# Beginning the block sums' transfers from GpSimd's queue, in a hybrid attention layer

## The chip, the cores and the metric

The kernel runs on one core of a Trainium2 chip. A core has TensorE (PE; its weight loads are listed as PEld), VectorE (DVE), ScalarE (ACT), GpSimd (POOL) and SyncE (SP), and 16 DMA engines that move data between HBM and the on-chip memory. Each engine works through its own instructions in order. A transfer is begun by an instruction that stands in the queue of one of the engines; that instruction waits there for its semaphores, and so does everything behind it on that engine. The metric is the device time of one execution in microseconds (us).

## The reference

One layer over 1024 tokens of width 1024, all in float32. A normalised input is projected to the columns of three mixers: a gated delta rule in both directions, grouped-query attention (8 query heads, 2 key heads) and cross-attention into 256 memory tokens (4 heads). Each mixer is projected, multiplied by a sigmoid gate and summed; an output projection and a squared-ReLU MLP follow.

```
y_att = block_gqa(aq, ak, av)
y_x = cross_attention(x_q, mk, mv)
merged = jnp.sum(gates * yb, axis=2)
x = x + merged @ w_out[l]
x = x + jnp.square(jax.nn.relu(hf @ w_up[l])) @ w_down[l]
return rms_norm(x, final_norm_w)
```

## The kernel before

The MLP's two products are done as Strassen-like sets of seven block products (P1 to P7). For the second one the kernel needs, beside blocks of `w_down`, four sums of blocks of it for each of 16 row pairs. It makes them early, in the attention stage, and keeps them in HBM in `wt_d[0..15]`, 128x4x512 each; they are read again only in the last stage (P6, P7, P4, P5).

The attention stage is a loop over 64 tiles `t` of 128 queries. Its TensorE order is pinned, so TensorE takes every product exactly in the order written. One pass of the loop does the scores of tile `t+2`, sometimes the output product of a pair (`q_out`), one step of the cross-attention generator `cross()`, some gate products as filling (`fill`), the turning of the probabilities (`q_trans`), and one call `block_sums(t // 4, t % 4)`.

`block_sums` fills a tile `wc` (128x4x128, two buffers in the pool `wcp`) by two loads from `w_down`, makes four subtractions on GpSimd in place (L1031), and stores the tile to `wt_d` by one transfer. There are 64 calls: 128 loads of 128 KB, 256 subtractions, 64 stores of 256 KB.

`cross()` goes through four heads, 16 passes each. A head begins by four loads into `mkv`, its keys and values; `mkv` has one buffer, so the loads must wait for the last product of the head before, which reads it. Two passes later TensorE needs it for the scores of the new head.

`ld` (L97) is the helper that begins a transfer from SyncE's queue; nearly every transfer of the kernel goes through it. The order in each queue is set by a scheduler, not by the order in which the code is written. Behind the attention come the rest of the gate products and the merge of the three branches, in the order 0, 2, 1: for the second and third of them GpSimd adds into `g_acc` (L1116), after VectorE has made the product in `g_l` (L1115). `g_l` has two buffers, loaded through SyncE's queue.

Of the kernel before, what the change touches and what calls it, by code (L numbers as in the profile page):

```python
# [86 lines left out]
def hybrid_block(tc, x, mem, mix_norm_w, w_in, dn_conv_w, dn_a_log, dn_dt_bias, dn_norm_w, q_norm_w, k_norm_w,  # L87
                 mem_norm_w, w_mem_kv, w_branch, w_out, ffn_norm_w, w_up, w_down, final_norm_w, ca_d, cb_d, rope_d,
                 out, dbg=None):
    nc = tc.nc  # L90
    pe, act, dve, gp = TensorE(tc), nc.scalar, nc.vector, nc.gpsimd
    def ld(out, in_):
        if out.dtype == F32R:
            out = out.bitcast(F32)
        if in_.dtype == F32R:
            in_ = in_.bitcast(F32)
        return nc.sync.dma_start(out=out, in_=in_)  # L97
# [100 lines left out]
    wt_d = [dram.tile([P, 4, 512], F32, name=f"wt_d{k}") for k in range(16)]  # L198
# [825 lines left out]
    def block_sums(k, c):  # L1024
        cs = slice(c * P, (c + 1) * P)
        w = wcp.tile([P, 4, P], F32, name="wc", tag="wc")
        for j in range(2):
            src = w_down[(2 * k + j) * P:(2 * k + j + 1) * P].rearrange("p (h c) -> p h c", h=2)
            ld(out=w[:, 2 * j:2 * j + 2], in_=src[:, :, cs])
        for o, a, b in ((0, 1, 0), (1, 3, 1), (3, 3, 0), (2, 2, 3)):  # L1030
            gp.tensor_tensor(out=w[:, o], in0=w[:, a], in1=w[:, b], op=ALU.subtract)  # L1031
        ld(out=wt_d[k][:, :, cs], in_=w)

    cr = cross()
    fill(24 * GATES[0])
# [7 lines left out]
    for t in range(NT):  # L1043
        if t + 2 < NT:
            q_scores(t + 2)
        if t % 2 == 0 and t:
            q_out(t // 2 - 1)
        next(cr, None)
        fill(FILL[0])
        q_trans(t, 0)  # L1050
        block_sums(t // 4, t % 4)
        fill(FILL[1])
        q_trans(t, 1)
        fill(FILL[2])
# [372 lines left out]
```

## Time and profile before

| | before |
|---|---|
| median of 3 runs | 1926.17 us (1922.19 to 1927.29) |
| the profiled execution's own time | 1923.72 us |
| its span in the profile | 1921.9 us |
| TensorE busy in the span | 1827.6 us (95%) |
| GpSimd busy | 532.4 us (28%) |
| packets of SyncE's DMA queue | 51.8% of 16 engines' span |

The span runs from the first to the last instruction seen; the execution's own time is 1.8 us longer. Busy shares are means over stages with different limits, so what a change in one stage does is to be read in that stage: the attention loop lies between about 588 and 1018 us.

### The profile page before, as it was taken

To read this page: it belongs to the slowest core of one execution; us is meant where nothing else is said; L and a number is where in the kernel's file an instruction comes from. 1 tells how busy PE (TensorE), PEld (TensorE's weight loads), DVE (VectorE), ACT (ScalarE), POOL (GpSimd) and SP (SyncE) were. 2 spreads that over 40 slices of the span, in tenths; PEclk is the share of its full clock that TensorE was granted. 3 is DMA by queue.
4 is the path that set the end of the run, shared out by engine and by line. 5 is a ranking of instruction groups with operands and counts; after the bars stand their busy time and mean duration, and the time that the engine had idled before them with its cause. 6 is when DMAs were issued, how large, how long until landed. Compare 5 with 4: busy or idle time off the path is not lost.

```text
span 1921.9 us, 27229 instructions
## 1 busy us (share of the span) xinstructions
PE 1827.6 (95%) x9891; PEld 1546.2 (80%) x9891; DVE 1237.4 (64%) x1795; ACT 808.2 (42%) x1597; POOL 532.4 (28%) x598
## 2 busy tenths in 40 slices
PE   6999999999999959869999999989999999999998
PEld 5888788988988848758888887867888888788886
DVE  4677989993676636646663456367787776555562
ACT  5453434653545636546663113133222223543341
POOL 1003131231343434442000052123656561011300
PEclk8999999998999979979999999999999999999999
DMA  7235664566656565564215545412454449666662
GB/s 152 71 106 165 196 200 138 160 181 187 186 150 197 167 187 171 179 190 146 88 55 167 201 150 183 135 66 80 147 179 142 159 174 350 240 206 201 203 198 66
DMA packets 340313, 313.28 MB, mean 163 GB/s; under 512 B 51986, under 2 KB 271314, under 8 KB 339667
## 3 DMA queue, kind: packets, MB, share of 16 engines
q1 hardware_dynamic: 339858, 311.02, 51.8%
q8 instruction: 78, 1.28, 0.3%
q10 hardware_dynamic: 320, 0.52, 0.1%
q14 instruction: 57, 0.46, 0.1%
HBM read 208.15 MB, written 103.32 MB: 162 GB/s over the span
## 4 chain that ended last, share of the span: by engine, by line
PE 82%; DMA 8%; DVE 5%; POOL 2%; issue 2%; ACT 1%; SPq 1%; POOLq 0%; ACTq 0%; DVEq 0%
PE ps L81 34%; PE ps_mm L81 30%; PE ps_dn L81 4%; PE ps_t L84 3%; PE ps_sm L81 3%; PE ps_t L81 2%; PE ps_s L81 2%; DMA wc<-in_w_down_dram 2%; PE ps_sp L81 2%; DMA wt_d<-wc 2%; SPq L97 1%; POOL wc L1031 1%; DMA xs_d<-dd 1%; DMA X<-xs_d 1%; DVE c_acc L412 1%
## 5 line engine op out<-in xcount | busy, mean ns | idle before, releaser
L81 PE MATMUL ps<-hs,ws 128*128 128x512 f32 x1344 | 312.6, 392 | 0.3 <-ACT hs L139 0.2
L81 PEld LDWEIGHTS ps<-hs,ws 128*128 128x128 f32 x1344 | 251.7, 189 | 52.0 <-ACT hs L139 0.8
L81 PE MATMUL ps_mm<-hTh,w_hi 128*128 128x512 f32 x704 | 286.6, 407 | 5.4 <-ACT hTh L139 4.8
L81 PE MATMUL ps_mm<-hTl,w_hi 128*128 128x512 f32 x704 | 284.4, 404 | 0.0
L81 PE MATMUL ps_mm<-hTh,w_lo 128*128 128x512 f32 x704 | 278.2, 395 | 3.1 <-DVE w_lo L140 3.1
L140 DVE TENSOR_TENSOR ab_lo<-ab_raw,ab_hi 128x1024 fp32r<-128x1024 f32 x112 | 139.7, 1296 | 94.4 <-issue 65.5
L1031 POOL TENSOR_TENSOR wc<-wc 128x128 f32<-128x128 f32 x256 | 127.7, 508 | 182.6 <-DMA wc<-in_w_down_dram 172.6
L139 ACT CAST ab_hi<-ab_raw 128x1024 fp32r<-128x1024 f32 x112 | 111.7, 1050 | 142.7 <-PE ps_mm L81 89.0
L81 PEld LDWEIGHTS ps_mm<-hTh,w_hi 128*128 128x128 f32 x704 | 134.3, 191 | 30.1 <-ACT hTh L139 5.0
L81 PEld LDWEIGHTS ps_mm<-hTh,w_lo 128*128 128x128 f32 x704 | 133.9, 190 | 29.1 <-DVE w_lo L140 3.3
L81 PEld LDWEIGHTS ps_mm<-hTl,w_hi 128*128 128x128 f32 x704 | 134.3, 191 | 20.8
L81 PE MATMUL ps<-ab_hi 128*128 128x512 f32 x336 | 129.9, 389 | 1.6 <-ACT ab_hi L139 1.6
L81 PE MATMUL ps<-ab_lo,ab_hi 128*128 128x512 f32 x336 | 130.6, 389 | 0.1
L81 PE MATMUL ps<-ab_hi,ab_lo 128*128 128x512 f32 x336 | 130.6, 389 | 0.0
L140 DVE TENSOR_TENSOR ptl<-ps_t,pth 128x512 fp32r<-128x512 f32 x128 | 86.5, 687 | 60.2 <-ACT pth L139 59.9
L139 ACT CAST w_hi<-w_raw 128x1024 fp32r<-128x1024 f32 x64 | 67.3, 1052 | 117.3 <-PE ps_mm L81 107.1
L140 DVE TENSOR_TENSOR w_lo<-w_raw,w_hi 128x1024 fp32r<-128x1024 f32 x64 | 83.0, 1298 | 41.6 <-ACT w_hi L139 40.7
L1116 POOL TENSOR_TENSOR g_acc<-g_acc,g_l 128x512 f32<-128x512 f32 x28 | 41.4, 1482 | 246.0 <-ACT g_yh L139 211.9
L139 ACT CAST pth<-ps_t 128x512 fp32r<-128x512 f32 x128 | 74.2, 586 | 51.1 <-PE ps_t L84 50.9
L901 DVE TENSOR_REDUCE nmx<-ps_s 128x1 f32<-128x1024 f32 x64 | 78.2, 1222 | 17.9 <-PE ps_s L81 17.0
L902 ACT ACTIVATE pm<-ps_s,nmx 128x1024 f32<-128x1024 f32 x64 | 71.7, 1120 | 41.1 <-DVE nmx L901 41.1
L84 PEld LDWEIGHTS ps_t<-ca,pm 128*128 128x128 f32 x512 | 64.1, 142 | 18.6 <-DVE cpl L140 1.4
(325 smaller groups left out, 4080.9 us busy)
## 6 DMA issues: line engine op xcount, KB each, us to landing
w_raw<-in_w_in_dram SPq DMA_DIRECT2D x50, 512.0 KB
ab_raw<-ab_d SPq DMA_DIRECT2D x96, 256.0 KB
w_raw<-in_w_up_dram SPq DMA_DIRECT2D x34, 512.0 KB
wc<-in_w_down_dram SPq DMA_DIRECT2D x128, 128.0 KB
wt_d<-wc SPq DMA_DIRECT2D x64, 256.0 KB
ab_d<-f_a SPq DMA_DIRECT2D x32, 512.0 KB
ab_raw<-wt_d SPq DMA_DIRECT2D x64, 256.0 KB
g_d<-gt SPq DMA_DIRECT2D x48, 256.0 KB
```

The costliest lines, as they stand in the source:

```text
L81: return self._put(self.tc.nc.tensor.matmul(*a, **k))
L84: return self._put(self.tc.nc.tensor.transpose(*a, **k))
L97: return nc.sync.dma_start(out=out, in_=in_)
L139: act.copy(out=hi, in_=src)
L140: (eng or dve).tensor_tensor(out=lo, in0=src, in1=hi.bitcast(F32), op=ALU.subtract)
L412: dve.scalar_tensor_tensor(out=acc[:, o], in0=xn[:, i], scalar=cw[:, ct, j:j + 1], in1=acc[:, o], op0=ALU.mult, op1=ALU.add)
L901: dve.tensor_reduce(out=nmx, in_=ps, axis=AX.X, op=ALU.max, negate=True)
L902: act.activation(out=p_out, in_=ps, func=AF.Exp, bias=nmx, accum_out=sm)
L1031: gp.tensor_tensor(out=w[:, o], in0=w[:, a], in1=w[:, b], op=ALU.subtract)
L1116: (dve if bi == 2 and mt > 5 else gp).tensor_tensor(out=acc[mt][:, c], in0=acc[mt][:, c], in1=t, op=ALU.add)
```

## The change

Three lines of `block_sums`: its loads and its store are begun by GpSimd (`gp`, which is `nc.gpsimd`) and no longer by SyncE.

```
     def block_sums(k, c):
...
         for j in range(2):
             src = w_down[(2 * k + j) * P:(2 * k + j + 1) * P].rearrange("p (h c) -> p h c", h=2)
-            ld(out=w[:, 2 * j:2 * j + 2], in_=src[:, :, cs])
+            gp.dma_start(out=w[:, 2 * j:2 * j + 2], in_=src[:, :, cs])
         for o, a, b in ((0, 1, 0), (1, 3, 1), (3, 3, 0), (2, 2, 3)):
             gp.tensor_tensor(out=w[:, o], in0=w[:, a], in1=w[:, b], op=ALU.subtract)
-        ld(out=wt_d[k][:, :, cs], in_=w)
+        gp.dma_start(out=wt_d[k][:, :, cs], in_=w)
```

The orders of TensorE, VectorE and ScalarE are the same in both kernels. Of SyncE's queue, this is the stretch ahead of the second cross-attention head's `mkv` loads, before:

```order
L97 DMA wt_d_204<-wc 512x1x128
L97 DMA qh<-qs_d 128x2x256
L97 DMA wc<-in_w_down_dram 128x2x128
L97 DMA wt_d_204<-wc 512x1x128
L97 DMA wc<-in_w_down_dram 128x2x128 x3
L97 DMA wt_d_205<-wc 512x1x128
L97 DMA g_d_0_93<-gt 128x512
L97 DMA wc<-in_w_down_dram 128x2x128
L97 DMA w_raw<-in_w_in_dram 128x8x128
L97 DMA mkv<-mk_d 128x256
```

The same stretch now:

```order
L97 DMA w_raw<-in_w_in_dram 128x8x128
L97 DMA g_d_0_93<-gt 128x512
L97 DMA y_d_125<-yt 128x256
L97 DMA qh<-qs_d 128x2x256
L97 DMA g_d_0_93<-gt 128x512
L97 DMA w_raw<-in_w_in_dram 128x8x128
L97 DMA mkv<-mk_d 128x256
```

The loads `wc` and the stores `wt_d` are gone from between the others; what is left stands in the order in which it stood.

On GpSimd, the end of the block sums was this before (256 subtractions between the last work of the delta rule, `o_rs`, and the merge, `g_acc`):

```order
L844 TENSOR_TENSOR oacc_4610<-oacc_4610,o 128x512
L854 TENSOR_TENSOR o_rs<-o_ss,mhalf 128x4
L1031 TENSOR_TENSOR wc<-wc 128x128 x256
L1116 TENSOR_TENSOR g_acc<-g_acc,g_l 128x512 x28
```

Now its queue holds the transfers too, and it ends so:

```order
L1029 DMA wc<-in_w_down_dram 128x2x128 x4
L1031 TENSOR_TENSOR wc<-wc 128x128 x8
L1032 DMA wt_d_213<-wc 512x1x128
L1032 DMA wt_d_214<-wc 512x1x128
L1029 DMA wc<-in_w_down_dram 128x2x128 x4
L1031 TENSOR_TENSOR wc<-wc 128x128 x8
L1032 DMA wt_d_214<-wc 512x1x128 x2
L1029 DMA wc<-in_w_down_dram 128x2x128 x2
L1031 TENSOR_TENSOR wc<-wc 128x128 x4
L1032 DMA wt_d_214<-wc 512x1x128
L1116 TENSOR_TENSOR g_acc<-g_acc,g_l 128x512 x28
```

Most of the 64 calls stand in pairs like the first two here: four loads, eight subtractions, two stores, in GpSimd's own queue and ahead of the merge's additions.

## Rows read from the trace of the kernel before

**Rows 1.** Busy time by stretch: start:end, length, PE, PEld, DVE, ACT, POOL, PEclk, DMA, GB/s

```profile
588.00:888.00 300.00, 258.71 (x1477) 221.17 (x1476) 174.21 (x274) 168.83 (x303) 127.72 (x256) 0.93 0.60 180
888.00:1030.00 142.00, 141.96 (x832) 121.83 (x831) 91.06 (x145) 88.45 (x158) 0.00 (x0) 1.00 0.29 93
```

**Rows 2.** Who waited for whom, 588 to 888: total us, times, longest

```profile
POOL wc L1031 <- DMA wc<-in_w_down_dram: 172.6, 77, 15.8
PE ps_mm L81 <- DMA mkv<-mk_d: 41.2, 2, 21.7
```

**Rows 3.** Timeline of PE: first scores of the four heads [idle before]

```profile
596.34 0.88 PE L81 MATMUL ps_mm<-mkv,cxq 128*128 128x256 f32 x6
...
712.04 1.99 PE L81 MATMUL ps_mm<-mkv,cxq 128*128 128x256 f32 x6 [19.50 <-DMA mkv<-mk_d]
...
832.78 2.06 PE L81 MATMUL ps_mm<-mkv,cxq 128*128 128x256 f32 x6 [21.75 <-DMA mkv<-mk_d]
...
931.02 0.88 PE L81 MATMUL ps_mm<-mkv,cxq 128*128 128x256 f32 x6
```

**Rows 4.** What SyncE's queue itself waited for, 588 to 888

```profile
SPq L97 <- POOL wc L1031: 76.8, 50, 3.8
SPq L97 <- DMA wt_d<-wc: 52.6, 38, 3.2
```

**Rows 5.** Timeline of SyncE's queue: the second head's first `mkv` load

```profile
707.43 0.58 SPq L97 DMA_DIRECT2D mkv<-mk_d  x1
```

**Rows 6.** Busy time by stretch, as Rows 1, behind the two waits

```profile
714.00:716.00 2.00, 2.00 (x9) 1.60 (x8) 1.36 (x4) 1.14 (x1) 1.02 (x3) 0.50 0.11 31
...
717.00:718.00 1.00, 1.00 (x6) 0.70 (x5) 0.73 (x3) 0.71 (x4) 0.38 (x1) 0.64 0.57 170
...
837.00:838.00 1.00, 1.00 (x5) 0.73 (x5) 0.37 (x1) 0.99 (x4) 0.35 (x2) 0.91 0.58 166
```

**Rows 7.** Timeline of PE and SyncE's queue ahead of the fourth head

```profile
919.74 0.39 PE L81 MATMUL ps_mm<-cph,mkv 128*128 128x512 f32 x1
...
920.16 0.32 SPq L97 DMA_DIRECT2D mkv<-mk_d  x1
...
921.94 0.43 SPq L97 DMA_DIRECT2D mkv<-mv_d  x1
```

**Rows 8.** The tile `wc`: count, ns min/median/max, first and last start

```profile
L1031 POOL TENSOR_TENSOR wc<-wc x256: 451/462/1457, 592.6 to 886.7; 128x128 f32<-128x128 f32 x128
L97 SPq DMA_DIRECT2D wc<-in_w_down_dram x128: 539/610/1482, 587.6 to 882.5; - x128
L97 SPq DMA_DIRECT2D wt_d<-wc x64: 555/567/573, 596.1 to 887.2; - x64
```

**Rows 9.** Timeline of SyncE's queue and POOL through one pair of calls

```profile
867.70 2.07 SPq L97 DMA_DIRECT2D wt_d<-wc  x2
...
870.49 2.57 SPq L97 DMA_DIRECT2D wc<-in_w_down_dram  x4
...
873.19 0.46 POOL L1031 TENSOR_TENSOR wc<-wc 128x128 f32<-128x128 f32 x1 [4.02 <-DMA wc<-in_w_down_dram]
```

**Rows 10.** POOL's groups by shape, 540 to 590: busy us, mean ns

```profile
L854 POOL TENSOR_TENSOR o_rs<-o_ss,mhalf 128x4 f32<-128x4 f32 x6 | 6.5, 1075 | 5.4 <-DVE o_ss L853 5.4
```

**Rows 11.** Timeline of DVE, POOL and SyncE's queue at the second branch

```profile
1100.92 0.69 DVE L1115 SCALAR_TENSOR_TENSOR g_l<-g_l,ps_mm 128x512 f32<-128x512 f32 x1 [0.72 <-PE ps_mm L81]
1103.64 0.69 DVE L1115 SCALAR_TENSOR_TENSOR g_l<-g_l,ps_mm 128x512 f32<-128x512 f32 x1 [2.03 <-PE ps_mm L81]
...
1109.14 0.69 DVE L1115 SCALAR_TENSOR_TENSOR g_l<-g_l,ps_mm 128x512 f32<-128x512 f32 x1 [0.38 <-issue]
...
1101.69 1.29 POOL L1116 TENSOR_TENSOR g_acc<-g_acc,g_l 128x512 f32<-128x512 f32 x1 [0.34 <-DVE g_l L1115]
...
1103.01 0.32 SPq L97 DMA_DIRECT2D g_l<-g_d  x1
```

**Rows 12.** DVE's groups by shape, 585 to 890: busy us, mean ns

```profile
L929 DVE TENSOR_SCALAR pm<-pm,rv 128x1024 f32<-128x1024 f32 x21 | 16.3, 775 | 0.7
```

More of the change, by code (lines that the diff above doesn't have):

```diff
@@ L1028, in block_sums @@
             src = w_down[(2 * k + j) * P:(2 * k + j + 1) * P].rearrange("p (h c) -> p h c", h=2)
-            ld(out=w[:, 2 * j:2 * j + 2], in_=src[:, :, cs])
+            gp.dma_start(out=w[:, 2 * j:2 * j + 2], in_=src[:, :, cs])
         for o, a, b in ((0, 1, 0), (1, 3, 1), (3, 3, 0), (2, 2, 3)):
             gp.tensor_tensor(out=w[:, o], in0=w[:, a], in1=w[:, b], op=ALU.subtract)
-        ld(out=wt_d[k][:, :, cs], in_=w)
+        gp.dma_start(out=wt_d[k][:, :, cs], in_=w)
     cr = cross()
```

## Prediction

> **What bounds the kernel now.** I read the busy time by stretch first. In the stretch of the block sums, 588 to 888 us, TensorE is busy for 258.7 of 300 us; in the next one, with the same loop and no block sums, for 141.96 of 142 [rows 1]. So the loop can keep TensorE full, and something beside the block sums takes 41 us from it. The list of waits names it: TensorE waited twice for a load of `mkv`, 41.2 us in all, the longest 21.7 [rows 2]. The timeline puts these waits at the first scores of the second and third cross-attention heads, with 19.50 and 21.75 us of idle time ahead of them; the first and fourth heads begin without one [rows 3].
>
> Why the load was late is seen in SyncE's queue. The second head's load was begun at 707.43 [rows 5], and TensorE went on at 712.04 [rows 3]: the transfer with its three companions took 4.6 us, the rest of the wait was time in the queue. In this stretch the queue waited 76.8 us for the subtractions on GpSimd and 52.6 us for stores of `wt_d` to land [rows 4]. Each of these waits holds all that stands behind it, and of the eleven transfers that the order shows ahead of `mkv`, eight are the block sums'. The fourth head is the counter-example in the same trace: with no block sums in the queue, its loads were begun at 920.16 to 921.94, right after the last product that reads the old tile (919.74) [rows 7], and its scores ran at 931.02 without a wait [rows 3]. From release to use there are 10.9 us, and the four loads need 4.6; so 6 us are to spare.
>
> **What the change gives.** It takes 192 transfers out of SyncE's queue (128 loads, 64 stores [rows 8]). The second and third heads' loads then stand as the fourth's do now, behind loads and stores that follow TensorE's own pace. I take both waits to go: 19.50 + 21.75 = 41.25 us.
>
> Behind each wait TensorE ran slower for a while. The granted clock was 0.50 (1.2 of 2.4 GHz) from 714 to 716, after 20 us with hardly a matmul, and 0.64 in the microsecond from 717 [rows 6], so it rose at about 717.3: 5.3 us at half speed, 2.6 us lost. After the second wait it rose in the microsecond from 837 [rows 6], at about 837.1: 4.3 us from 832.78, 2.15 lost. Together 4.75.
>
> A cross-check by the distances between first scores [rows 3]: 115.70, 120.74 and 98.24 us. Less the idle time and the half-speed loss that fall in each (19.50; 21.75 + 2.6; 2.15) they are 96.2, 96.4 and 96.1. Nothing else in the loop is late, so there is no further gain: **41.25 + 4.75 = 46.0 us**. Behind the loop the work hangs on TensorE and moves forward with it.
>
> **What the change costs.** GpSimd had waited 172.6 us for the loads and worked 127.7 us [rows 1, 2]. Now it must also begin 192 transfers, and while it waits at one (for a store to land, so that the buffer is free) it can't subtract. The queue's order gives the time of a pair of calls. Say a load costs GpSimd L and a store S to begin.
>
> - Four loads: 4 L. The first load that could go had to wait for the first store.
> - The last load landing: 2.1 us. SyncE began the load at 870.49, which takes 0.6, and the first subtraction ran at 873.19 [rows 9].
> - Subtractions left then: about five of eight, at 127.72 / 256 = 0.50 us [rows 1], 2.5 us.
> - The first store: S to begin and 2.2 us to land (from 867.70, less 0.57 [rows 8], to the next load at 870.49 [rows 9]).
>
> In sum 4 L + S + 6.8 us. With SyncE's prices (0.61 and 0.57 [rows 8]) that is 9.8; the pairs took (886.7 + 0.5 - 592.6) / 32 = 9.2 [rows 8], so the formula is a little high.
>
> This work must end before GpSimd is needed again, by the second branch of the merge. There the second addition ended at 1102.98, and the load into the same `g_l` buffer was begun at 1103.01, VectorE using it at 1109.14 [rows 11]. Products come 2.72 us apart [rows 11] into two buffers, so TensorE would feel VectorE at about 1109.0 + 2.72 = 1111.7; VectorE was done with this one at 1109.83: 1.9 us to spare. The block sums may thus end at 1102.98 + 1.9 - 2 x 1.29 = 1102.3, on the old clock, and 46 us earlier, at 1056, on the new. From 588 that is 468 us, **14.6 us a pair**: 4 L + S up to 7.8, some 1.55 us for each transfer. Each microsecond beyond is one lost, since TensorE waits for the merge; the gain is eaten at 1102, 16.1 us a pair, 4 L + S = 9.3, some 1.85 each.
>
> No row shows a transfer begun by GpSimd. From below, L is SyncE's 0.32 when nothing crowds it [rows 7]; from above, the whole of a load from its beginning to its use, 2.7, and of a store, 2.8 [rows 9]. The row that I find nearest is GpSimd's own `o_rs`, 1.08 us for 4 values a partition [rows 10], an instruction that is nearly all fixed price. I take L = 1.0, and S = 1.5, since the store's target has 512 runs where the load has 256. Then a pair takes 4.0 + 1.5 + 6.8 = 12.3 us, 32 pairs 394 us, and the block sums end at 982: 74 us early, cost nothing. At the upper ends a pair takes 10.8 + 2.8 + 6.8 = 20.4, they end at 1241, 185 us late, and 139 us are lost.
>
> The buffer that `wcp` frees is taken by the tiles `g_t`, used behind 1300 us, and `wt_d` is read in the last stage only, so neither sets an earlier date. The traffic is the same; it is spread over more time, where the DMA engines had 0.60 and later 0.29 of their time taken [rows 1].
>
> The profile's row of busy DMA time, 0.60, says that the engines were not full while `mkv` waited [rows 1]. The Trainium skill, DMA: Bandwidth & Descriptors, section Rules for kernel authors, says that spreading transfers over several issuing engines doesn't help bandwidth, as all run on the same DMA engines, and saves only issue time. By that rule alone the sum would be 0; it is the second rival below. The same page's Specifications give about 1 us to the first byte for a transfer from GpSimd and 0.6 from SyncE; an estimate from that page adds 0.4 to each of the two landings, 13.1 a pair, and changes nothing here.
>
> **Rivals.**
>
> *GpSimd becomes the bound.* Place: the block sums' last pairs, ahead of the first `g_acc`. For it: a price that no row shows, paid 192 times in a row with 6.8 us of unavoidable waits in each pair. It decides from 1.85 us a transfer. At 2.0 for loads and 2.5 for stores a pair is 17.3, they end at 1142, 86 us late: 1926 - 46 + 86 = 1966. At the ends above, 2065. Against it: 0.46 to 1.08 us is what GpSimd takes for small instructions [rows 8, 10]. VectorE may hold GpSimd up too: if each of the 21 `pm` scalings (16.3 us [rows 12]) stopped it wholly, 0.5 us a pair would come on top, which isn't enough alone. The Trainium skill, SBUF — State Buffer, section SBUF: two separate sides, describes such a stop of GpSimd's descriptor writing by VectorE's two-port operations; no row before shows one.
>
> *The loads come no earlier.* The wait would then be in the transfers or in other entries of the queue: TensorE waits as now, about 1924. For it: other stores wait there for ScalarE and VectorE. Against it: the fourth head. The rule on issuing engines (DMA: Bandwidth & Descriptors) would make this of the change.
>
> *Late, but not by much.* 1.55 to 1.85 us a transfer: the gain is partly given back, 1886 to 1920.
>
> **How the numbers follow.** The profiled time 1923.72 less 46.0 is 1877.7; the median shown is 2.45 above it, so I predict 1880, with 1874 to 1886 as the range of this case alone. Chances: the full gain 0.66; late but still faster 0.10; no earlier loads or a draw 0.05; GpSimd as the bound, slower, 0.19. The range 1873 to 1935 takes in all but most of the last case. Faster by over 0.3% (about what a measurement can tell here): 0.66 + 0.10 = 0.76; same 0.05; slower 0.19.
>
> **What would show it.** Right: no wait of TensorE for `mkv`, a granted clock of 1.00 through the loop, first scores 96 us apart, GpSimd's block sums over 12 to 13 us a pair, ending at about 980, and `g_acc` waiting for VectorE. Wrong: block sums running beyond 1056 and `g_acc`, then VectorE's `g_l` and TensorE waiting behind them. Transfers begun from GpSimd at over 1.85 us would make the kernel slower.

## The result, and the profile after

| | before | changed |
|---|---|---|
| median | 1926.6 us (1922.19 to 1927.29, 4 runs) | 1876.67 us (1869.89 to 1880.57, 4 runs) |
| ratio to before | | 0.9742, 95% interval 0.971 to 0.9774 |
| span of the profiled execution | 1921.9 us | 1874.7 us |
| granted clock, mean | 0.977 | 0.992 |

The change makes the kernel 2.6% faster: 49.9 us by the medians, 47.2 us by the two profiled spans. The forecast was 1880 us.

The busy time by stretch of the changed kernel, over the whole of the loop (columns as in [rows 1]), and below it the first scores of the four cross-attention heads in TensorE's timeline:

```profile
588.00:990.00 402.00, 401.57 (x2335) 344.68 (x2334) 270.20 (x421) 258.37 (x463) 262.05 (x442) 1.00 0.52 169
```

```profile
592.39 0.87 PE L81 MATMUL ps_mm<-mkv,cxq 128*128 128x256 f32 x6
...
688.87 0.88 PE L81 MATMUL ps_mm<-mkv,cxq 128*128 128x256 f32 x6
...
784.79 0.88 PE L81 MATMUL ps_mm<-mkv,cxq 128*128 128x256 f32 x6
...
880.70 0.88 PE L81 MATMUL ps_mm<-mkv,cxq 128*128 128x256 f32 x6
```

TensorE is busy for 401.57 of 402 us at a granted clock of 1.00, where it had been busy for 258.71 of 300 at 0.93 [rows 1]. No first score has an idle time in brackets behind it, where two had [rows 3]. The heads follow each other by 96.5, 95.9 and 95.9 us. From the first to the fourth it is 288.31 us, and was 334.68 [rows 3]: 46.4 us of the 47.2 are won here.

The second head's load in SyncE's queue, and the last product that reads the old tile:

```profile
676.89 0.62 PE L81 MATMUL ps_mm<-cph,mkv 128*128 128x512 f32 x2
677.59 0.39 PE L81 MATMUL ps_mm<-cph,mkv 128*128 128x512 f32 x1
```

```profile
678.01 0.32 SPq L97 DMA_DIRECT2D mkv<-mk_d  x1
```

The load is begun 0.4 us after the last product that reads the old tile has started (677.59), and 10.9 us before the scores need it (688.87). The wait has not moved elsewhere: it is gone.

What GpSimd pays, by the tile `wc` (columns as in [rows 8]):

```profile
L1031 POOL TENSOR_TENSOR wc<-wc x256: 448/462/1542, 585.6 to 957.3; 128x128 f32<-128x128 f32 x128
L1029 POOL DMA_DIRECT2D wc<-in_w_down_dram x128: 702/720/1034, 580.5 to 953.2; - x128
L1032 POOL DMA_DIRECT2D wt_d<-wc x64: 697/740/888, 589.2 to 958.1; - x64
```

To begin a load costs GpSimd 0.72 us, a store 0.74. The block sums run from 585.6 to 958.9, which is 11.65 us a pair, where SyncE's queue had needed 9.2 [rows 8]. So they take 27% longer, and nobody waits for them. What GpSimd waited for (588 to 1000), and its first addition in the merge:

```profile
POOL wc L1029 <- DMA wt_d<-wc: 61.7, 36, 4.7
POOL wc L1031 <- DMA wc<-in_w_down_dram: 34.9, 44, 2.0
```

```profile
1049.01 2.28 POOL L1116 TENSOR_TENSOR g_acc<-g_acc,g_l 128x512 f32<-128x512 f32 x1 [90.17 <-ACT g_yh L139]
```

GpSimd stood idle for 90 us between the last store and this addition, so the block sums could have ended at least that much later.

### The profile page after: what moved, and what is told of

Its sections match the earlier page's. It is cut to its first block, busy times and chain, and to the rows that moved or that the text cites. A ratio compares the mean times of both kernels' runs of the same rounds, so it can differ in the third digit from the quotient of the medians.

```text
span 1874.7 us, 27160 instructions
## 1 busy us (share of the span) xinstructions
PE 1820.7 (97%) x9891; PEld 1541.5 (82%) x9891; DVE 1244.3 (66%) x1795; ACT 807.1 (43%) x1597; POOL 674.0 (36%) x790
## 3 DMA queue, kind: packets, MB, share of 16 engines
q0 software_dynamic: 11264, 33.57, 5.2%
## 4 chain that ended last, share of the span: by engine, by line
PE 86%; DVE 5%; DMA 4%; issue 2%; ACT 2%; SPq 1%; POOL 0%; POOLq 0%; ACTq 0%; DVEq 0%
PE ps L81 33%; PE ps_mm L81 33%; PE ps_t L84 4%; PE ps_dn L81 3%; PE ps_t L81 3%; PE ps_sm L81 3%; PE ps_s L81 3%; PE ps_sp L81 2%; DMA xt<-in_x_dram 1%; DMA w_raw<-in_w_out_dram 1%; SPq L97 1%; DVE c_acc L412 1%; DMA w_raw<-in_w_mem_kv_dram 1%; DMA xs_d<-dd 1%; PE ps_mm L84 1%
## 5 line engine op out<-in xcount | busy, mean ns | idle before, releaser
L81 PEld LDWEIGHTS ps<-hs,ws 128*128 128x128 f32 x1344 | 252.1, 189 | 51.8 <-ACT hs L139 0.8
L139 ACT CAST ab_hi<-ab_raw 128x1024 fp32r<-128x1024 f32 x112 | 111.8, 1050 | 147.3 <-PE ps_mm L81 84.7
L1029 POOL DMA_DIRECT2D wc<-in_w_down_dram x128 | 92.1, 725 | 74.5 <-DMA wt_d<-wc 61.7
```

The lines of the kernel that those rows point to most:

```text
L81: return self._put(self.tc.nc.tensor.matmul(*a, **k))
L139: act.copy(out=hi, in_=src)
L1029: gp.dma_start(out=w[:, 2 * j:2 * j + 2], in_=src[:, :, cs])
```

## The experiments

The kernel before, run again beside the experiments, took 1924.02 to 1926.1 us by its medians. The theories at the start:

- **A, the order.** The `mkv` loads are late because of where they stand in SyncE's order. Between the first call of block sums and the second head's loads there are 26 whole calls, and between those and the third head's another 26 (counted in the order), while TensorE needs the loads after 16 passes. A call took (886.7 + 0.5 - 592.6) / 64 = 4.6 us [rows 8] and a pass 96 / 16 = 6. So 26 calls take 120 us where TensorE comes after 96: 587.6 + 26 x 4.6 = 707.2, and the load was begun at 707.43 [rows 5].
- **B, the queue.** SyncE's queue is overloaded, and any relief of it helps.
- **C, the transfers.** What counts is how the transfers run on the DMA engines when GpSimd begins them.

**Only the `mkv` loads moved to GpSimd's queue.** The block sums stay on SyncE; the loads stand behind 104 and 208 subtractions, which are again 26 and 52 calls.

```
-                ld(out=mkv[:, i], in_=mk_d[i][:, h])
-                ld(out=mkv[:, 2 + i], in_=mv_d[i][:, h].rearrange("p k d -> p (k d)"))
+                gp.dma_start(out=mkv[:, i].bitcast(F32), in_=mk_d[i][:, h])
+                gp.dma_start(out=mkv[:, 2 + i].bitcast(F32), in_=mv_d[i][:, h].rearrange("p k d -> p (k d)"))
```

> Block sums as in the kernel before (loads and stores begun from SyncE), only the 16 loads of mkv are begun from GpSimd. In the order of GpSimd's queue the second and third heads' loads then stand behind 104 and 208 subtractions, that is 26 and 52 calls of block_sums. Theory A (the load is late because it stands in order behind some 26 calls, at 4.6 us a call, while TensorE needs it after 16 passes of 6 us): 26 x 4.6 = 120 us, the waits of about 20 us stay, time 1915 to 1930. Theory B (it is SyncE's queue, so any load taken out of it comes in time): waits gone, 1875 to 1885.

Measured: 1928.53 us, ratio 1.0015 (0.9999 to 1.0032). TensorE's wait at the second head stays (18.31 us and 3.12 behind it, where it was 19.50 [rows 3]), though these loads have left SyncE's queue:

```profile
705.16 0.58 PE L81 MATMUL ps_mm<-mkv,cxq 128*128 128x256 f32 x1 [18.31 <-DMA mkv<-mk_d]
```

At the third head, too, TensorE waits (23.14 us). Another queue in which they stand behind the same calls changes nothing. That speaks for A and against B.

**Half of the change: the loads alone, and the stores alone.** In the first, `wc` is loaded from GpSimd's queue and stored from SyncE's; in the second the other way round. Each is one of the two edits of the change.

> Only the 128 loads of the block sums begun from GpSimd, the 64 stores from SyncE as before. 20, 39 and 59 stores stand ahead of the second, third and fourth heads' mkv loads. Theory A: a call takes about 5.2 us (4 x 0.72 + 2.1 + 2.5 + 0.57 + 2.2 = 10.3 a pair), so the second load is begun at about 588 + 104 = 692, some 8 us late, the others some 3 to 9 us: waits of 10 to 25 us in all, time 1890 to 1905. Theory B: the queue is freed by two thirds, waits gone or down to about 14 us, 1877 to 1893. If only the traffic mattered (theory C): as after, 1877.

> Only the 64 stores of the block sums begun from GpSimd, the 128 loads from SyncE as before. 46 and 92 loads, 23 and 46 calls, stand ahead of the second and third heads' mkv loads. Theory A: about 4.9 us a call, so the second load is begun at about 588 + 113 = 701, waits of about 17 and 14 us and two stretches at half speed: 1905 to 1918. Theory B: the queue is freed by one third, waits of about 27 us, 1905 to 1912. Theory C (traffic): as after or as before, no value between.

Measured: loads alone 1921.15 us, ratio 0.9995 (0.9978 to 1.0011); stores alone 1912.58 us, 0.9941 (0.9921 to 0.9961). The second is as A expected, the first is not: 20 us and more were expected from it, and nothing that can be measured came. TensorE's wait at the second head, with the loads alone and then with the stores alone on GpSimd:

```profile
696.07 0.55 PE L81 MATMUL ps_mm<-mkv,cxq 128*128 128x256 f32 x1 [7.03 <-DMA mkv<-mk_d]
```

```profile
701.32 2.08 PE L81 MATMUL ps_mm<-mkv,cxq 128*128 128x256 f32 x6 [12.36 <-DMA mkv<-mk_d]
```

The miss is one of the time of a call, not of the mechanism. With the loads alone the block sums spread so far that the fourth head waits as well. The tile `wc` of that kernel, and its fourth head in TensorE's timeline:

```profile
L1031 POOL TENSOR_TENSOR wc<-wc x256: 442/461/1500, 585.9 to 949.4; 128x128 f32<-128x128 f32 x128
L1029 POOL DMA_DIRECT2D wc<-in_w_down_dram x128: 720/720/992, 580.6 to 943.2; - x128
```

```profile
922.96 0.58 PE L81 MATMUL ps_mm<-mkv,cxq 128*128 128x256 f32 x1 [16.20 <-DMA mkv<-mk_d]
```

With each kernel's own time of a call, theory A gives the time of the second head's load. The calls ahead are counted in the order, the start is that of the first load into `wc`:

| kernel | calls ahead | us a call | expected start of the load | seen |
|---|---|---|---|---|
| before | 26 | 4.60 | 587.6 + 119.6 = 707.2 | 707.43 |
| loads alone on GpSimd | 20 | 5.69 | 580.6 + 113.8 = 694.4 | 691.44 |
| stores alone on GpSimd | 23 | 5.01 | 583.5 + 115.2 = 698.7 | 694.79 |

The same working gives the third heads' loads closer still: 826.8, 802.5 and 814.0 expected (52, 39 and 46 calls), 828.45, 802.33 and 814.37 seen. Since the time of a call is measured afterwards, this bears out the count of the calls ahead; the time itself had been forecast too short. Fewer calls stand ahead in the loads-alone kernel, but each takes longer: three heads wait, 37.4 us in all, where two waited 41.2 [rows 2]. Half of the 192 transfers had left SyncE's queue by bytes and two thirds by number, and nothing was won, so B falls here too. C would have had half of the effect at least in one of the two, in proportion to what GpSimd began; 0 and 13 us for two thirds and one third of the transfers speak against it.

**Only the order, all from SyncE's queue.** The block sums' transfers and the `mkv` loads are held in the order in which the program writes them, so that 17, 33 and 49 calls stand ahead of the three heads' loads.

```
-                ld(out=mkv[:, i], in_=mk_d[i][:, h])
+                tc.keep_in_program_order(ld(out=mkv[:, i], in_=mk_d[i][:, h]))
...
-            ld(out=w[:, 2 * j:2 * j + 2], in_=src[:, :, cs])
+            tc.keep_in_program_order(ld(out=w[:, 2 * j:2 * j + 2], in_=src[:, :, cs]))
...
-        ld(out=wt_d[k][:, :, cs], in_=w)
+        tc.keep_in_program_order(ld(out=wt_d[k][:, :, cs], in_=w))
```

> All transfers begun from SyncE as in the kernel before; only their order in the queue is kept as the program has it for the block sums and the mkv loads, so that 17, 33 and 49 calls stand ahead of the second, third and fourth heads' loads instead of 26, 52 and 64. Theory A: 17 x 4.6 = 78 us, less than the 96 us of a head, the waits go: 1875 to 1890. Theory B (SyncE's queue is the cause, whatever its order) and theory C (traffic of the DMA engines): the waits stay, 1915 to 1930.

Measured: 1902.28 us, ratio 0.9889 (0.9868 to 0.991). Just under half of the gain, with nothing taken from SyncE's queue; B and C had none. But A had more. SyncE's queue and TensorE at the second head:

```profile
691.91 0.43 SPq L97 DMA_DIRECT2D mkv<-mk_d  x1
...
694.39 0.55 PE L81 MATMUL ps_mm<-mkv,cxq 128*128 128x256 f32 x1 [4.31 <-DMA mkv<-mk_d]
```

The old tile had been free since 678.63, when its last product began, but the program writes the loads of a head in the very pass that needs them. They are begun at 691.91, and TensorE comes at 690.1: 1.8 us of its wait lie ahead of the beginning and 2.5 are the transfer. Three heads do this, 4.3 us each, with a stretch at half speed behind each (a granted clock of 0.50 from 697 to 701). Up to the fourth head's scores this makes 19.3 us (307.6 against 288.4 in the next run), of the 26.2 by which this kernel's span is the longer; the rest comes behind them. A's sum had failed at the time of a call: 17 calls took 97 us here (from the first load into `wc` at 594.6) and not 78.

**The order, and the loads written earlier.** As the last, and the loads of a head are written right behind the last product that reads the old tile (the helper `head(h)` holds the four loads).

```
                 gemm(po, [(mvh[:, k], mvl[:, k], cph[:, k], cpl[:, k]) for k in range(2)])
+                if f == 1 and h < 3:
+                    nxt = head(h + 1)
```

> Everything still from SyncE's queue; the block sums' transfers and the mkv loads keep the program's order there, and a head's mkv loads are written right behind the last product of the head before (one pass and more earlier than in the run on the order alone, where each of three heads still waited 4.3 us for the load's own duration). Theory A: the three waits of 4.3 us and their half-speed stretches go: 1876 to 1888 us, TensorE waiting for no mkv. Rival B (SyncE's queue has to be freed): as the run on the order alone, 1898 to 1906 us or slower.

Measured: 1877.3 us, ratio 0.9751 (0.9722 to 0.9779): the time of the changed kernel (1876.67), with all 192 transfers still begun by SyncE. The load and the scores of the second head, the loop's busy time, and the page's DMA queues:

```profile
683.78 0.58 SPq L97 DMA_DIRECT2D mkv<-mk_d  x1
```

```profile
691.45 0.88 PE L81 MATMUL ps_mm<-mkv,cxq 128*128 128x256 f32 x6
```

```profile
588.00:990.00 402.00, 401.88 (x2334) 344.22 (x2333) 268.71 (x421) 258.78 (x465) 134.20 (x256) 1.00 0.55 169
```

```profile
q1 hardware_dynamic: 339858, 311.02, 53.0%
```

The load is begun 7.7 us ahead of its use, and TensorE never waits. The queue's packets and bytes are those of before (339858, and 311.02 MB), so neither a relief of SyncE's queue nor the way in which GpSimd's transfers run is needed for the gain. TensorE, VectorE and ScalarE take their instructions in the same order as in the kernel before and in the changed one, so no other reordering made it either. Theory A is shown; B and C fall.

**The transfers begun from ScalarE's queue.** `act.dma_start` where the change has `gp.dma_start`: SyncE is as free as in the changed kernel.

> Block sums' 192 transfers begun from ScalarE's queue instead of GpSimd's; nothing else. Theory A (the second matrix's head loads were late because some 26 calls of block sums stood ahead of them in SyncE's order): SyncE is as free as in the changed kernel, so TensorE waits for no mkv load, and the 46 us are won; what is lost is what ScalarE's own order now holds up: each load waits in it for the store of a buffer, with a softmax row or a cast of the attention queued behind. ScalarE works 258 of 402 us in this stage; 192 beginnings of some 0.6 us make it 373, and the same waits of about 3 us a pair would fill it. Expected 1890 to 1960 us with TensorE waiting for ScalarE (ps_s, pth) and not for mkv. Rival D (what counts is only that the transfers leave SyncE, the queue they go to has room): 1872 to 1882 us.

Measured: 1955.27 us, ratio 1.0164 (1.013 to 1.0198). No wait of TensorE for `mkv` is left, and yet it is slower than before. The tile `wc`, what ScalarE waited for (580 to 1050), and the loop's busy time:

```profile
L1029 ACTq DMA_DIRECT2D wc<-in_w_down_dram x128: 547/600/1397, 577.7 to 885.6; - x128
```

```profile
ACT pth L139 <- POOL wc L1031: 14.6, 8, 3.9
...
ACT pm L902 <- POOL wc L1031: 9.7, 3, 3.7
...
ACT pth L139 <- DMA wt_d<-wc: 9.7, 5, 3.4
```

```profile
588.00:990.00 402.00, 349.41 (x1891) 286.60 (x1891) 220.68 (x353) 215.27 (x388) 120.45 (x252) 0.96 0.49 149
```

A cast of `pth` has no use for a subtraction on GpSimd; it stands behind a store that has. TensorE gets through 1891 products in the 402 us where it got through 2335. From first to fourth head this kernel needs 368.0 us (590.31 to 958.27), the changed one 288.3: 79.7 us, which is the 78.6 us between the two medians. Which queue gets the waits matters as much as which queue loses them. How the 79.7 us divide is not shown: ScalarE also begins 192 transfers more, and the scheduler put 66 of its other instructions and 71 of VectorE's in another place between 585 and 811 us.

**GpSimd slowed down, by one and by three operations a call.** They multiply the tile `wc` by one, ahead of its store (once, or `range(3)`).

```
+        for _ in range(1):
+            gp.tensor_scalar(out=w, in0=w, scalar1=1.0, scalar2=None, op0=ALU.mult)
```

> The changed kernel with one more GpSimd operation in each of the 64 calls of block sums (a 128x512 multiplication by one, in place). At 0.55 to 1.5 us each (bounds by the nearest GpSimd rows) a pair takes 11.65 + 1.1 to 3.0 = 12.8 to 14.7 us, the block sums end at 995 to 1055, just inside the deadline of the first g_acc at 1049. Theory (slack on GpSimd up to the merge is free): 1872 to 1885 us. Rival (GpSimd's pace bounds the stage already): 64 x 0.55 to 1.5 = 35 to 96 us slower, 1912 to 1973.

> The changed kernel with three such operations in each call. A pair takes 11.65 + 3.3 to 9 = 15 to 20.6 us, the block sums end at 1065 to 1246 and so 15 to 200 us behind the deadline of 1049; the 28 additions to g_acc and with them TensorE's work come later by this, less what the 1.5 us additions catch up. Theory (deadline as predicted): 1885 to 2060 us, TensorE waiting in the merge and not in the attention; the time above 1877 equals the lateness at the first g_acc within some 15 us. Rival (the merge has slack of its own): 1872 to 1885 us.

Measured: one 1894.71 us, three 2022.71 us. Three operations came out in the theory's range. One misses both expectations: it cost 18 us. It takes 1.58 us in the mean, and the block sums end at 1072, later than the 1055 that was allowed for. The tile and TensorE's waits:

```profile
L1034 POOL DMA_DIRECT2D wt_d<-wc x64: 737/766/942, 592.2 to 1071.3; - x64
```

```profile
PE ps_mm L81 <- ACT g_yh L139: 10.4, 2, 9.6
PE ps_mm L81 <- DVE g_acc L1115: 2.9, 1, 2.9
```

```profile
1000.00:1040.00 40.00, 25.97 (x83) 18.46 (x82) 15.88 (x15) 10.96 (x11) 23.70 (x32) 0.74 0.71 233
```

These rows are of the kernel with one operation, the last of them its busy time from 1000 to 1040. The heads still follow each other by 96 us, so GpSimd's pace does not bound the loop. The loss is between 1000 and 1040, where TensorE waits for `g_yh`, of the merge's first products; ScalarE waits there for `y_raw` loads from SyncE's queue. No wait of TensorE or ScalarE there names GpSimd. The orders say why: the added operations led the scheduler to another order of TensorE, ScalarE, VectorE and SyncE in the merge. SyncE's first `y_raw` loads, in the changed kernel and with one operation:

```profile
966.21 2.58 SPq L97 DMA_DIRECT2D y_raw<-y_d  x3
```

```profile
1005.37 11.83 SPq L97 DMA_DIRECT2D y_raw<-y_d  x6
```

In the changed kernel they stand ahead of stores of `g_d` that wait for ScalarE, here behind them, so they are begun 39 us later.

To tell order from pace, one more kernel has a small operation in the place of the big one: a power of 4 values a partition, its result unused. TensorE's, ScalarE's and VectorE's orders are then the same as with the one big operation, row for row.

```
+            gp.tensor_tensor(out=mhalf[:, 60:64], in0=w[:, 0, 0:4], in1=mhalf[:, 0:4], op=ALU.pow)
```

> The changed kernel with one small GpSimd operation of about 1.06 us (a power of 4 values a partition, its result unused) in each call of block sums in place of the 1.58 us one of the run with one operation a call. TensorE's, ScalarE's and VectorE's orders are the same row for row as in that run, and differ from the changed kernel's in the merge. A pair takes 11.65 + 2.1 = 13.8 us, so the block sums end at about 1026, ahead of the first g_acc. If the 18 us of that run came from its order in the merge (TensorE waiting for g_yh near 1002): the same time again, 1888 to 1899 us. If they came from GpSimd's pace (the block sums ended at 1072, 23 us behind the first g_acc of the changed kernel): 1874 to 1882 us.

Measured: 1893.2 us, ratio 0.9834 (0.9805 to 0.9864).

```profile
L1034 POOL DMA_DIRECT2D wt_d<-wc x64: 712/740/1145, 593.0 to 1011.7; - x64
```

```profile
1066.05 2.31 POOL L1118 TENSOR_TENSOR g_acc<-g_acc,g_l 128x512 f32<-128x512 f32 x1 [53.59 <-ACT g_yh L139]
```

The block sums end 54 us ahead of the first addition, and the 16.5 us above the changed kernel are lost all the same: they belong to the order above all. The first `y_raw` load is begun at 998.07 here. These loads come 32 us later than in the changed kernel by their place in the queue; that the block sums' last transfers, begun until 1011.7, slowed them besides is not excluded. The further 60 us by which the big operation delays the block sums (1071.3 against 1011.7) cost 1.5 us, less than the runs of one kernel differ by.

The kernel with three operations does run past the deadline. Its first addition on GpSimd, and TensorE behind it:

```profile
1198.53 4.95 POOL L1118 TENSOR_TENSOR g_acc<-g_acc,g_l 128x512 f32<-128x512 f32 x4
```

```profile
1205.37 0.80 PE L81 MATMUL ps_mm<-g_yh,w_hi 128*128 128x512 f32 x1 [118.53 <-DVE g_l L1117]
```

TensorE stands still for 118.5 us, from 1086.8, waiting for `g_l`, which waits for GpSimd. The block sums' end at 1198.5 was thus 118.5 us too late: on this kernel's clock the deadline was 1080.0. The same product of TensorE in the changed kernel:

```profile
1061.57 0.39 PE L81 MATMUL ps_mm<-g_yh,w_hi 128*128 128x512 f32 x1
```

That is 25.2 us earlier, which puts the deadline at 1054.8 on the changed kernel's clock. Of the 130.8 us by which this kernel's span (2022.4) is above that of the small operation (1891.6), 8.2 had come about ahead of this wait, 4.7 of them before the loop (first scores at 596.69 and 592.00).

## Why the prediction was right

- **The gain.** Predicted: both waits go, 41.25 us, and 4.75 us at half speed behind them, 46.0. From first to fourth head 46.4 us were won. The half-speed term was read slightly low: a mean clock of 0.64 in the microsecond from 717 [rows 6] puts the rise at 717.7 and not at 717.3, which makes the term 5.0 and the sum 46.2. The loads were begun right behind the last product that reads the old tile and 10.9 us before use, as was read off the fourth head.
- **The cause of the late load.** The prediction put it down to the entries of the block sums ahead in SyncE's queue, and held the waits of that queue (76.8 and 52.6 us [rows 4]) against it. That is right, but it is only half: what makes the load late is that 26 calls were put ahead of a load that is needed after 16 passes. The order alone, put right, gives the whole gain from SyncE's own queue (1877.3 us).
- **The cost on GpSimd.** Both prices were over-estimated: L is 0.72 us, not 1.0; S is 0.74, not 1.5. The guess that a store's price grows with its number of runs failed. The row taken for L, `o_rs`, was called nearly all fixed price; but a subtraction on 128 values a partition takes GpSimd only 0.46 [rows 8], so that could not be read off it. With the measured prices the formula 4 L + S + 6.8 gives 10.4 us a pair, and 11.65 were measured. So the fixed part was too low, by 1.2 us, and the two errors partly cancelled: predicted 12.3 us and an end at 982, measured 11.65 and 959. That the end came near is in part luck; that it came well ahead of the deadline is not.
- **The deadline.** 1056 was predicted for the end of the block sums; the kernel with three operations gives 1055 by the working above. TensorE stops at the product that the prediction named (about 1111.7 in the kernel before, where it ran at 1111.60). The product came 50.0 us earlier in the changed kernel and not 46, and the room was 2.5 us larger than read (1104.8 against 1102.3 on the old clock), so the nearness to 1056 is partly luck. GpSimd as the bound, the rival that would have made it slower, is real, and its point of decision was about right; the price of a transfer was far from it.
- **The loads come no earlier.** That was the rival by the rule on issuing engines in the Trainium skill, DMA: Bandwidth & Descriptors, Rules for kernel authors, that spreading transfers over engines helps no bandwidth. The trace agrees with the rule as far as it goes: the loop's traffic is 169 GB/s in the changed kernel and 169 with everything on SyncE. But no bandwidth was missing; a load stood in the wrong place of an in-order queue.
- **The rest.** The changed kernel's first scores come 3.95 us earlier than before (592.39 against 596.34 [rows 3]), ahead of any block sum that could have mattered. The prediction had nothing of it. It lies mostly in the granted clock of stages ahead of the loop, before and in the changed kernel:

```profile
530.00:546.00 16.00, 14.47 (x102) 13.47 (x102) 11.24 (x29) 5.49 (x16) 9.03 (x8) 0.79 0.56 161
```

```profile
530.00:546.00 16.00, 14.77 (x133) 13.72 (x132) 13.15 (x36) 8.11 (x24) 9.36 (x8) 1.00 0.69 197
```

From 80 to 95 us it was 0.89 and 1.00. The kernel with the early loads, all from SyncE, has 1.00 from 80 to 95 and 0.79 from 530 to 546, and its first scores come at 595.16. Nothing of the change stands there, and why the clock differed is open. Behind the fourth head 46.4 + 3.95 - 47.2 = 3.1 us are given back; at least part of it is the clock again, 0.88 from 1598 to 1612 where it had been 1.00 from 1645 to 1660. That the two nearly cancel is luck.

## What to carry to other kernels

A load that comes late is first to be looked for in its queue's order: count the work that the order puts ahead of it, multiply by the time of each, and compare with when it is needed. Another queue for the work ahead, or another place for the load in the same queue, can then give the same gain (1876.67 and 1877.3 us here); take the queue whose engine has a long idle stretch, since the waits go with the transfers (GpSimd: nothing lost; ScalarE: 78.6 us, in part perhaps by its changed order). And an experiment that adds instructions can change the scheduler's order far away: compare the orders before putting its time down to what was added.

## What had not been expected of the hardware

The same 192 transfers make far fewer packets when GpSimd begins them. The changed kernel's DMA queues (packets, MB, share of 16 engines' span):

```profile
q1 hardware_dynamic: 271250, 277.45, 47.3%
q0 software_dynamic: 11264, 33.57, 5.2%
```

SyncE's queue had 339858 packets with 311.02 MB and has 68608 packets and 33.57 MB less; the same bytes are 11264 packets in GpSimd's. (Begun from ScalarE they are 68608 packets again.) That is 489 bytes a packet against 2980. It won no time here: the two shares together are 52.5% of 1874.7 us, 984 us, where SyncE's queue alone took 51.8% of 1921.9, 996 us.

GpSimd's price to begin a transfer is nearly the same for 128 KB from 256 runs (0.72 us) and for 256 KB to 512 runs (0.74), and hardly varies: the longest of 128 loads took 1.03 us, while VectorE worked for 270 of 402 us beside it. The Trainium skill, SBUF — State Buffer, SBUF: two separate sides, tells of a stop of GpSimd's descriptor writing by VectorE's two-port operations. The trace shows no beginning held up for as long as a `pm` scaling takes (0.83 us in the mean here): the 32 that overlap one took 0.75 us in the mean. Four of the five longest loads (0.78 to 1.03) are among them, so a shorter hold-up is possible; no row shows the descriptor writing itself, nor whether the scalings are such operations.
